# First q chunks copied out of PSUM before their rotation, their norms placed within later products, and some squares and weight sums on GpSimd

## Chip, cores and metric

The kernel runs on one core of a Trainium2 chip, as one program. The metric is the device time of that program in microseconds (us); lower is better. Engines are named as in the profile: TensorE (PE, with its weight loads as PEld), VectorE (DVE), ScalarE (ACT), GpSimd (POOL) and SyncE (SP, which issues the DMA transfers). Each engine works through its own list of instructions in a fixed order, and semaphores hold an instruction until what it needs is there.

## What is computed

A two-layer trunk over 1024 prompt frames and 32 sample frames, model width 1024: layer 0 mixes by retention, layer 1 by gated linear attention (GLA), each followed by a convolutional FFN (2 x 2816 wide), with RMS norms ahead of each part and a last norm. Cut to what the change touches:

```python
def rmsnorm(x, g):
    y = x * lax.rsqrt(jnp.mean(x * x, axis=-1, keepdims=True) + EPS)
    return y * g

def rotary(x, pos):                       # on q and k of each retention head
    x1, x2 = x[..., :half], x[..., half:]
    return concatenate([x1 * cos - x2 * sin, x1 * sin + x2 * cos])

def conv_ffn(h, conv_state, w_up, conv_w, conv_b, w_down):
    u = h @ w_up                          # then a causal convolution over 3 frames
    ...
    return (silu(gate) * val) @ w_down, ext[:, T:]

def trunk(...):
    for i in range(DEPTH):
        x = x + mixer(rmsnorm(x, norm_mix[i]))
        x = x + conv_ffn(rmsnorm(x, norm_ffn[i]), ...)
    return rmsnorm(x, norm_final), ...
```

## The kernel before

Everything is float32, kept transposed: features on the 128 partitions (eight tiles `kt`), frames along the free axis. A product of float32 values is made of three matmuls: each operand is split into a rounded high part and a low remainder (`hi`, `lo`; `whi` by a ScalarE cast at L102 and `wlo` by a VectorE subtraction at L103; for the activations `XA` at L146 on ScalarE and L147 on VectorE), and hi x hi, hi x lo and lo x hi add up in PSUM (L120, L121, L122). So each weight tile and each activation tile costs ScalarE one instruction and VectorE one before TensorE can use it.

The mixing parts work in three chunks of frames, `CM`: 384, 384 and 288 wide; the FFN's up-projection in four quarters of 264 (`TH`), two quarters to a half `s`.

**The start.** `retention()` (L258) loads the transposed input in three chunks `xc` and the first two weight tiles of head 0's q (`w01`). Then, for each chunk `c`: every `kt` is split (`split_x`, L144 to L147) and squared (`sumsq`, L126 to L142). The square is on ScalarE for even `kt` (L131) and on VectorE for odd `kt` (L129); the squares are added up in two `ss` tiles, on VectorE for even and on GpSimd for odd `kt` (L142), from a ring of two `sq` buffers. `rot_proj` makes the chunk's q in a PSUM pair `pj` (two of them exist). `rms_a` (L152) sums the squares over partitions (`pn`, L160), goes through a short chain of 128x3 operations (L167 to L172) and makes a diagonal matrix `dg` (L174); `rms_b` (L178) multiplies it by ones (`pr`, L180) and copies the row of reciprocal roots to `R` (L182, ScalarE). The norm is put into the rotation's factors: `cos` and `sin` of the chunk are multiplied by `R` (L312, L313, VectorE), and `rot` (L274) multiplies q, read from PSUM, by them (`tc` L281, `ts` L282, VectorE) and makes the rotated `qk` from those two on GpSimd (L284, L285). After the three chunks the pool `rp` is opened, `rotary(0, 1)` makes k of head 0 in the same way, and the loop over the nine blocks of 128 frames begins, with `pss` (L353) as its first matmul.

**The FFN.** `ffn_up` (L926) makes the up-projection in a scheme of seven products instead of eight for each pair of column tiles `f` (22 of them) and half `s`. Sums of activation blocks are made by `x_sums` (L906: `minus` at L918, the split at L913 on ScalarE and L914 on VectorE, into `XA` and `XB`), and sums of weight blocks by `weight_sums(f)` (L930): two tiles `rg` and `rv` are loaded, `rg` is split (`wgh`, `wgl`), and four additions or subtractions of 128x512 (L943, L944, L945, L949) and two more splits (`wsh`/`wsl`, `wth`/`wtl` at L938 on ScalarE, L939 on VectorE) follow; `wv` (L947, L948) splits one half of `rv`. Products (L987, L991, L992) leave PSUM by ScalarE copies (L966) and VectorE additions (L962). The first quarters' residual additions (L1115), norm (`pn`, `dg`, `pr` at L1126) and scaling by the norm (L1139) are still running on VectorE when `weight_sums(0)` and `weight_sums(1)` are made.

The instruction order of each engine is fixed when the program is built, by the order of the text and a scheduler that takes dependences and buffers into account; `order(ins, after)` adds a dependence without a wait, to hold an instruction behind another in that order.

Of the kernel before, what the change touches and what calls it, by code (L numbers as in the profile page):

```python
# [9 lines left out]
F32 = mybir.dt.float32  # L10
# [40 lines left out]
def trunk_kernel(ctx: ExitStack, tc: tile.TileContext, io):  # L51
# [63 lines left out]
    def proj(ps, w, c0, n):  # L115
        hi, lo = w
        for kt in range(KT):
            k = slice(kt * P, kt * P + P)
            rh = xh[:, kt, c0:c0 + n]
            PE.matmul(ps, hi[:, k], rh, start=kt == 0, stop=False)  # L120
            PE.matmul(ps, hi[:, k], xl[:, kt, c0:c0 + n], start=False, stop=False)  # L121
            PE.matmul(ps, lo[:, k], rh, start=False, stop=kt == KT - 1)  # L122

    def sumsq(ss, kt, src, n, on_dve=False):  # L126
        def square(dst):
            if on_dve:
                V.tensor_tensor(dst, src, src, op=ALU.mult)  # L129
            else:  # L130
                S.activation(dst, src, AF.Square)  # L131

        s_ = ss[kt % len(ss)]
        if kt < len(ss):
            square(s_[:, :n])
            if n < 384:
                G.memset(s_[:, n:], 1.0)
        else:
            sq = nps[0].tile([P, 384], F32, tag="sq", name=f"sq{uid()}", bufs=2)
            square(sq[:, :n])  # L140
            eng = V if kt % 2 == 0 else G
            eng.tensor_tensor(s_[:, :n], s_[:, :n], sq[:, :n], op=ALU.add)  # L142
# [34 lines left out]

    def rms_b(dg, c, ps, copy=True):  # L178
        c0, n = CM[c]
        PE.matmul(ps[:, :n], ones, dg.rearrange("p m t -> p (m t)")[:, :n], start=True, stop=True)  # L180
        if copy:
            S.copy(R[:, c0:c0 + n], ps[:, :n])  # L182

    def new_ss(depth=1):
        return [nps[0].tile([P, 384], F32, tag="ss", name=f"ss{uid()}", bufs=2 * depth) for _ in range(2)]
# [72 lines left out]
    def retention():  # L258
# [5 lines left out]
        def rsm(name):  # L264
            return pp.tile([P, 512], F32, tag="sm", name=name, bufs=2)

        def rot_proj(w, c):
            c0, n = CM[c]
            ps = pp.tile([P, 2, 512], F32, tag="pj", name=f"pj{uid()}", bufs=2)
            for d in range(2):  # L270
                proj(ps[:, d, :n], w[d], c0, n)
            return ps

        def rot(ps, c, j):  # L274
# [14 lines left out]
        with pool("x0", bufs=3, side="right") as xp, pool("x0n", side="right") as nps[0]:  # L289
            for c, (c0, n) in enumerate(CM):  # L290
                xc = xp.tile([P, KT, 384], F32, tag="xc", name=f"xc{c0}")
                step = 2 if c == 0 else 8
                for kt in range(0, KT, step):
                    nc.sync.dma_start(xc[:, kt:kt + step, :n], io["xT"][:, kt:kt + step, c0:c0 + n])
                    if c == 0 and kt in (0, 6):
                        w01.append(load_w(io["w_rqk"][0, kt // 6]))
                xs.append(xc)
            ones_ident()
            cos = const("cos", [P, T], pl=rk)
            sin = const("sin", [P, T], pl=rk)  # L300
            rmask = const("rmask", [P, RH, P], pl=rk)
            rcol = const("rcol", [P, RH, 4], pl=rk)
            qs0 = []
            for c, (c0, n) in enumerate(CM):
                ss = new_ss(2)
                for kt in range(KT):
                    split_x(0, xs[c][:, kt, :n], kt, c0, n)
                    sumsq(ss, kt, xs[c][:, kt, :n], n, kt % 2)
                ps = rot_proj(w01, c)
                dg = rms_a(ss, c, pp.tile([P, 512], F32, tag="sm", name=f"pn{uid()}", bufs=2), True)  # L310
                rms_b(dg, c, pp.tile([P, 512], F32, tag="sm", name=f"pr{uid()}", bufs=2))
                V.tensor_tensor(cos[:, c0:c0 + n], cos[:, c0:c0 + n], R[:, c0:c0 + n], op=ALU.mult)  # L312
                V.tensor_tensor(sin[:, c0:c0 + n], sin[:, c0:c0 + n], R[:, c0:c0 + n], op=ALU.mult)  # L313
                qs0.append(rot(ps, c, 0))
        rp = es.enter_context(pool("rp"))

        def rotary(h, j):
            w = [load_w(io["w_rqk"][h, 2 * j + d]) for d in range(2)]
            return [rot(rot_proj(w, c), c, j) for c in range(3)]

        def split_state(st):
            i = uid()
# [583 lines left out]
    def x_sums(X, x1, x2):  # L906
# [7 lines left out]
                V.tensor_tensor(X[o][:, 1], v, X[o][:, 0].bitcast(F32), op=ALU.subtract)  # L914
            return run

        def minus(d, a, b):
            return lambda: V.tensor_tensor(d, a, b, op=ALU.subtract)  # L918

        if x2 is None:  # L920
            return [split(1, b11), split(2, b21)]
        return ([minus(b12, b12, b11), split(5, b12)],
                [split(3, b22), minus(b22, b22, b12), split(6, b22),
                 minus(b11, b22, b11), split(7, b11), minus(b21, b22, b21), split(4, b21)])

    def ffn_up(l, X, todo, fc, sm, early, after):  # L926
        cw, cc, cst, room = fc
# [2 lines left out]
        def weight_sums(f):  # L930
# [9 lines left out]
                return h, l_  # L940

            g = split(rg, "wg")
            V.tensor_tensor(rv[:, a], rv[:, a], rv[:, b], op=ALU.add)  # L943
            V.tensor_tensor(rg[:, a], rv[:, a], rg[:, a], op=ALU.subtract)  # L944
            V.tensor_tensor(rg[:, b], rg[:, b], rg[:, a], op=ALU.subtract)  # L945
            v = w_tile(f"wv{uid()}")
            S.copy(v[:, a], rv[:, b])  # L947
            V.tensor_tensor(v[:, b], rv[:, b], v[:, a].bitcast(F32), op=ALU.subtract)  # L948
            V.tensor_tensor(rv[:, b], rv[:, b], rg[:, a], op=ALU.subtract)  # L949
            s2 = split(rg, "ws")  # L950
            s1 = split(rv, "wt")
            W[f] = {1: (g[0][:, a], g[1][:, a]), 2: (g[0][:, b], g[1][:, b]),
# [416 lines left out]
```

## Time and profile before

| | |
|---|---|
| time, median of 3 runs | 2928.82 us (2928.03 to 2929.93) |
| the profiled execution's own time | 2924.91 us |
| its span | 2923.1 us |
| mean granted TensorE clock | 0.995 |
| retention's first blocks begin (first L353) | 74.48 us |
| up-projection of the FFNs begins | about 944 us and 2184 us |

How to read it: times in a timeline are us from the start of the span; a row gives start, duration, engine, line, operation, `out<-in`, shapes, the count of instructions put together in the row, and in brackets the idle time before it with the instruction that ended it. Durations overlap somewhat within an engine: the next instruction of VectorE may start about 0.08 us before the last one ends, so what an instruction costs is the distance from its start to the next start. In a list of waits a row gives the waiting instruction, what it waited for, and the total, the number and the longest of the waits in us. A group gives its count, busy time and mean in ns of one, and then the idle time before it.

### The profile page before, as it was taken

What the parts mean: (1) busy time and instruction counts of PE and PEld (TensorE: products, weight loads), DVE (VectorE), ACT (ScalarE), POOL (GpSimd) and SP (SyncE); (2) the same over time, 40 slices, a digit from 0 to 9 for tenths busy, and PEclk for the clock granted to TensorE, in tenths of its full rate; (3) what the DMA queues carried; (4) which work ended last, traced back from release to release, by engine and by line L of the source; (5) the groups of instructions that cost most, each with busy time, mean ns of one, the idle gap of its engine ahead of it and who ended that gap; (6) DMA issues with size and microseconds to landing.
All of it is one profiled execution on the core that took longest, in us unless ns stands there. A gap on an engine that the chain in (4) does not pass through costs nothing.

```text
span 2923.1 us, 50853 instructions
## 1 busy us (share of the span) xinstructions
PE 2874.0 (98%) x20390; PEld 2776.0 (95%) x20390; DVE 1872.5 (64%) x3143; ACT 1248.0 (43%) x2238; POOL 328.9 (11%) x560
## 2 busy tenths in 40 slices
PE   8999999999999999999999999999999999999998
PEld 7888889899999999999999999999999999999998
DVE  7545464544477877777555577774488777775553
ACT  4424242422355444444444455553354444444443
POOL 3010101000011111111000032220010111110000
PEclk9999999999999999999999999999999999999999
DMA  4120211254656121222754401114642222227543
GB/s 153 37 88 28 86 57 57 90 173 164 217 183 213 59 87 72 84 79 75 260 181 170 166 21 50 50 43 152 216 155 73 81 74 82 73 86 242 183 161 125
DMA packets 168108, 339.69 MB, mean 116 GB/s; under 512 B 23712, under 2 KB 106784, under 8 KB 167872
## 3 DMA queue, kind: packets, MB, share of 16 engines
q1 hardware_dynamic: 167328, 335.87, 33.6%
q8 instruction: 159, 2.61, 0.4%
q14 instruction: 77, 0.63, 0.1%
q10 hardware_dynamic: 544, 0.59, 0.1%
HBM read 263.93 MB, written 72.47 MB: 115 GB/s over the span
## 4 chain that ended last, share of the span: by engine, by line
PE 90%; DVE 5%; ACT 2%; issue 1%; DMA 1%; POOL 1%; SPq 0%; DVEq 0%; ACTq 0%; POOLq 0%
PE pu L992 10%; PE pu L987 10%; PE pu L991 10%; PE pd L860 8%; PE pd L861 8%; PE pd L862 8%; PE pg L120 3%; PE pg L121 3%; PE pg L122 3%; PE pj L120 3%; PE pj L122 3%; PE pj L121 3%; PE psv L203 2%; PE psv L201 2%; PE psv L202 2%; PE pl L586 1%
## 5 line engine op out<-in xcount | busy, mean ns | idle before, releaser
L103 DVE TENSOR_TENSOR wlo<-raw,whi 128x1024 fp32r<-128x1024 f32 x258 | 324.8, 1260 | 283.4 <-ACT whi L102 277.4
L102 ACT CAST whi<-raw 128x1024 fp32r<-128x1024 f32 x258 | 269.9, 1049 | 482.2 <-PE pd L861 252.4
L860 PE MATMUL pd<-hh,whi 128*128 128x384 f32 (+1 forms) x880 | 284.7, 323 | 0.0
L862 PE MATMUL pd<-hh,wlo 128*128 128x384 f32 (+1 forms) x880 | 284.1, 323 | 0.0
L861 PE MATMUL pd<-hl,whi 128*128 128x384 f32 (+1 forms) x880 | 283.9, 323 | 0.1
L966 ACT COPY AR<-pu 128x264 f32<-128x264 f32 x264 | 99.1, 375 | 308.9 <-PE pu L992 306.5
L120 PE MATMUL pj<-XA,whi 128*128 128x384 f32 (+1 forms) x576 | 189.7, 329 | 11.4 <-ACT whi L102 7.4
L121 PE MATMUL pj<-XA,whi 128*128 128x384 f32 (+1 forms) x576 | 190.0, 330 | 2.4 <-DVE XA L147 2.2
L122 PE MATMUL pj<-XA,wlo 128*128 128x384 f32 (+1 forms) x576 | 188.4, 327 | 0.2 <-DVE wlo L103 0.2
L120 PE MATMUL pg<-XA,whi 128*128 128x352 f32 x576 | 186.0, 323 | 0.0
L121 PE MATMUL pg<-XA,whi 128*128 128x352 f32 x576 | 184.6, 320 | 0.0
L122 PE MATMUL pg<-XA,wlo 128*128 128x352 f32 x576 | 184.5, 320 | 0.0
L861 PEld LDWEIGHTS pd<-hl,whi 128*128 128x128 f32 x880 | 165.2, 188 | 0.8 <-DVE hl L837 0.4
L860 PEld LDWEIGHTS pd<-hh,whi 128*128 128x128 f32 x880 | 165.2, 188 | 0.5
L862 PEld LDWEIGHTS pd<-hh,wlo 128*128 128x128 f32 x880 | 165.2, 188 | 0.1
L860 PE MATMUL pd<-XB,whi 128*128 128x264 f32 x576 | 165.1, 287 | 0.0
L862 PE MATMUL pd<-XB,wlo 128*128 128x264 f32 x576 | 164.1, 285 | 0.0
L861 PE MATMUL pd<-XB,whi 128*128 128x264 f32 x576 | 164.0, 285 | 0.0
L1021 DVE SCALAR_TENSOR_TENSOR AR<-AR,cw 128x1058 f32<-128x1058 f32 x88 | 115.9, 1317 | 72.5 <-ACT AR L1020 72.5
L142 POOL TENSOR_TENSOR ss<-ss,sq 128x264 f32<-128x264 f32 (+2 forms) x48 | 50.8, 1058 | 929.3 <-ACT sq L131 906.7
L992 PE MATMUL pu<-XA,wgl 128*128 128x264 f32 x528 | 150.0, 284 | 0.0
L987 PE MATMUL pu<-XA,wgh 128*128 128x264 f32 x528 | 149.8, 284 | 0.0
(356 smaller groups left out, 9225.7 us busy)
## 6 DMA issues: line engine op xcount, KB each, us to landing
raw<-w_down SPq DMA_DIRECT2D x120, 512.0 KB, 3.6
raw<-w_ro SPq DMA_DIRECT2D x55, 512.0 KB, 3.8
rg<-w_up SPq DMA_DIRECT2D x44, 512.0 KB, 3.5
rv<-w_up SPq DMA_DIRECT2D x44, 512.0 KB, 3.4
scr_h<-AR SPq DMA_DIRECT2D x44, 512.0 KB, 2.6
AR<-scr_h SPq DMA_DIRECT2D x84, 192.0 KB, 3.8
raw<-w_go SPq DMA_DIRECT2D x23, 512.0 KB, 4.3
AR<-scr_or SPq DMA_DIRECT2D x16, 528.0 KB, 5.5
```

What stands on the lines that cost most here:

```text
L102: S.copy(hi, raw)
L103: V.tensor_tensor(lo, raw, hi.bitcast(F32), op=ALU.subtract)
L120: PE.matmul(ps, hi[:, k], rh, start=kt == 0, stop=False)
L121: PE.matmul(ps, hi[:, k], xl[:, kt, c0:c0 + n], start=False, stop=False)
L122: PE.matmul(ps, lo[:, k], rh, start=False, stop=kt == KT - 1)
L860: PE.matmul(o, w[0][:, k], h[0][:, :n], start=i == 0, stop=False)
L861: PE.matmul(o, w[0][:, k], h[1][:, :n], start=False, stop=False)
L862: self.last_mm = PE.matmul(o, w[1][:, k], h[0][:, :n], start=False, stop=i == nk - 1)
L987: mm = PE.matmul(ps, wh[:, k], x[:, 0, kt], start=m in (1, 2, 4, 5) and kt == 0, stop=False, skip_group_check=True)
L991: PE.matmul(ps, wh[:, k], x[:, 1, kt], start=False, stop=False, skip_group_check=True)
L992: mm = PE.matmul(ps, wl[:, k], x[:, 0, kt], start=False, stop=kt == 3, skip_group_check=True)
L1021: V.scalar_tensor_tensor(cj, uj[:, 1:T + 3], cw[:, nt, 1:2], cj, op0=ALU.mult, op1=ALU.add)
```

## The change

Three edits.

1. In the start, each of the first three q chunks is copied from PSUM, unrotated, by ScalarE into an SBUF tile. The norm of chunk c is made within the product of chunk c + 1 (`norm_first` after the first half, `norm_last` after the second, held there with `order`), and that of chunk 2 within the first chunk of k, which is projected before the pool `rp` is opened (`ahead_k`). The rotation reads the SBUF copy.
2. `sumsq` in these three chunks makes the squares of odd `kt` on GpSimd instead of VectorE. (Its other callers do not pass the argument.)
3. In the FFN, the four weight sums of `f` = 0 and 1 are made on GpSimd, and the subtraction that makes `b21` also, which is moved ahead of the split of product 6.

```diff
             PE.matmul(ps, hi[:, k], xl[:, kt, c0:c0 + n], start=False, stop=False)
-            PE.matmul(ps, lo[:, k], rh, start=False, stop=kt == KT - 1)
+            mm = PE.matmul(ps, lo[:, k], rh, start=False, stop=kt == KT - 1)
+        return mm
...
-    def sumsq(ss, kt, src, n, on_dve=False):
+    def sumsq(ss, kt, src, n, on_pool=False):
         def square(dst):
-            if on_dve:
-                V.tensor_tensor(dst, src, src, op=ALU.mult)
+            if on_pool:
+                G.tensor_tensor(dst, src, src, op=ALU.mult)
             else:
                 S.activation(dst, src, AF.Square)
...
     def rms_b(dg, c, ps, copy=True):
         c0, n = CM[c]
-        PE.matmul(ps[:, :n], ones, dg.rearrange("p m t -> p (m t)")[:, :n], start=True, stop=True)
+        mm = PE.matmul(ps[:, :n], ones, dg.rearrange("p m t -> p (m t)")[:, :n], start=True, stop=True)
         if copy:
             S.copy(R[:, c0:c0 + n], ps[:, :n])
+        return mm
...
-        def rot_proj(w, c):
+        def rot_proj(w, c, last_norm=False):
             c0, n = CM[c]
             ps = pp.tile([P, 2, 512], F32, tag="pj", name=f"pj{uid()}", bufs=2)
             for d in range(2):
-                proj(ps[:, d, :n], w[d], c0, n)
+                mm = proj(ps[:, d, :n], w[d], c0, n)
+                if last_norm:
+                    (norm_last if d else norm_first)(2, mm)
             return ps
...
+            stage = {}
+
+            def norm_first(c, after):
+                stage[c] = rms_a(stage[c], c, rsm(f"pn{uid()}"), True, after)
+
+            def norm_last(c, after):
+                c0, n = CM[c]
+                order(rms_b(stage[c], c, rsm(f"pr{uid()}")), after)
+                V.tensor_tensor(cos[:, c0:c0 + n], cos[:, c0:c0 + n], R[:, c0:c0 + n], op=ALU.mult)
+                V.tensor_tensor(sin[:, c0:c0 + n], sin[:, c0:c0 + n], R[:, c0:c0 + n], op=ALU.mult)
+                qs0[c] = rot(qs0[c], c, 0)
+
             for c, (c0, n) in enumerate(CM):
-                ss = new_ss(2)
+                stage[c] = new_ss(2)
                 for kt in range(KT):
                     split_x(0, xs[c][:, kt, :n], kt, c0, n)
-                    sumsq(ss, kt, xs[c][:, kt, :n], n, kt % 2)
-                ps = rot_proj(w01, c)
-                dg = rms_a(ss, c, pp.tile([P, 512], F32, tag="sm", name=f"pn{uid()}", bufs=2), True)
-                rms_b(dg, c, pp.tile([P, 512], F32, tag="sm", name=f"pr{uid()}", bufs=2))
-                V.tensor_tensor(cos[:, c0:c0 + n], cos[:, c0:c0 + n], R[:, c0:c0 + n], op=ALU.mult)
-                V.tensor_tensor(sin[:, c0:c0 + n], sin[:, c0:c0 + n], R[:, c0:c0 + n], op=ALU.mult)
-                qs0.append(rot(ps, c, 0))
+                    sumsq(stage[c], kt, xs[c][:, kt, :n], n, kt % 2)
+                ps = pp.tile([P, 2, 512], F32, tag="pj", name=f"pj{uid()}", bufs=2)
+                mm = proj(ps[:, 0, :n], w01[0], c0, n)
+                if c:
+                    norm_first(c - 1, mm)
+                mm = proj(ps[:, 1, :n], w01[1], c0, n)
+                q = rk.tile([P, 2, 384], F32, tag="qk0", name=f"qk{uid()}", bufs=3)
+                S.copy(q[:, :, :n], ps[:, :, :n])
+                qs0.append(q)
+                if c:
+                    norm_last(c - 1, mm)
+            wk = [load_w(io["w_rqk"][0, 2 + d]) for d in range(2)]
+            ahead_k = [(wk, rot_proj(wk, 0, True))]
         rp = es.enter_context(pool("rp"))

         def rotary(h, j):
-            w = [load_w(io["w_rqk"][h, 2 * j + d]) for d in range(2)]
-            return [rot(rot_proj(w, c), c, j) for c in range(3)]
+            w, ps = ahead_k.pop(0) if h == 0 else ([load_w(io["w_rqk"][h, 2 * j + d]) for d in range(2)], None)
+            return [rot(ps if ps and c == 0 else rot_proj(w, c), c, j) for c in range(3)]
...
-        def minus(d, a, b):
-            return lambda: V.tensor_tensor(d, a, b, op=ALU.subtract)
+        def minus(d, a, b, eng=V):
+            return lambda: eng.tensor_tensor(d, a, b, op=ALU.subtract)
...
-                [split(3, b22), minus(b22, b22, b12), split(6, b22),
-                 minus(b11, b22, b11), split(7, b11), minus(b21, b22, b21), split(4, b21)])
+                [split(3, b22), minus(b22, b22, b12), minus(b21, b22, b21, G), split(6, b22),
+                 minus(b11, b22, b11), split(7, b11), split(4, b21)])
...
-            V.tensor_tensor(rv[:, a], rv[:, a], rv[:, b], op=ALU.add)
-            V.tensor_tensor(rg[:, a], rv[:, a], rg[:, a], op=ALU.subtract)
-            V.tensor_tensor(rg[:, b], rg[:, b], rg[:, a], op=ALU.subtract)
+            E = G if f < 2 else V
+            E.tensor_tensor(rv[:, a], rv[:, a], rv[:, b], op=ALU.add)
+            E.tensor_tensor(rg[:, a], rv[:, a], rg[:, a], op=ALU.subtract)
+            E.tensor_tensor(rg[:, b], rg[:, b], rg[:, a], op=ALU.subtract)
...
-            V.tensor_tensor(rv[:, b], rv[:, b], rg[:, a], op=ALU.subtract)
+            E.tensor_tensor(rv[:, b], rv[:, b], rg[:, a], op=ALU.subtract)
```

In the changed kernel the lines move: the scheme's first matmul `pss` is L377 there, L120 to L122 stay.

## Prediction

> **What bounds the kernel now.** I read the page first, its busy shares and the chain that ended last.
>
> ```profile
> span 2923.1 us, 50853 instructions
> PE 2874.0 (98%) x20390; PEld 2776.0 (95%) x20390; DVE 1872.5 (64%) x3143; ACT 1248.0 (43%) x2238; POOL 328.9 (11%) x560
> PE 90%; DVE 5%; ACT 2%; issue 1%; DMA 1%; POOL 1%; SPq 0%; DVEq 0%; ACTq 0%; POOLq 0%
> ```
>
> TensorE is busy for all but 49 us, and the change takes no matmul away (it issues the same 19308 TensorE rows in another order). It can therefore win only where TensorE waits. Busy time by stretch (us; busy of PE, PEld, DVE, ACT, POOL; the granted clock is the third column from the right) shows where that is, inside the two regions that the diff touches:
>
> ```profile
> 10.00:20.00 10.00, 7.87 (x37) 6.82 (x37) 10.00 (x15) 6.54 (x13) 4.37 (x3) 1.00 1.07 364
> 20.00:30.00 10.00, 9.03 (x54) 8.35 (x53) 8.83 (x20) 6.72 (x17) 4.45 (x5) 1.00 0.53 202
> 30.00:40.00 10.00, 8.26 (x47) 7.06 (x46) 10.00 (x21) 2.04 (x4) 3.89 (x4) 0.95 0.07 15
> 40.00:50.00 10.00, 8.14 (x41) 7.69 (x39) 9.35 (x11) 2.37 (x3) 6.94 (x7) 0.71 0.11 36
> 50.00:60.00 10.00, 10.00 (x59) 9.65 (x59) 7.70 (x15) 4.45 (x10) 2.77 (x2) 1.00 0.65 222
> 960.00:975.00 15.00, 12.52 (x94) 11.54 (x94) 13.77 (x17) 8.44 (x11) 0.00 (x0) 1.00 0.11 36
> 2170.00:2190.00 20.00, 17.03 (x135) 16.38 (x133) 18.65 (x37) 10.46 (x18) 2.73 (x3) 1.00 0.59 207
> ```
>
> From 10 to 50 us VectorE is busy 10.0, 8.83, 10.0 and 9.35 of each 10 us and TensorE never full: the start is bound by VectorE. After 50 TensorE is full. In 40 to 50 the clock is 0.71, so the waits there are paid twice. The two FFN windows say the same: TensorE short, VectorE at 13.77 of 15 and 18.65 of 20. The list of TensorE's waits between 7 and 80 us names the late work:
>
> ```profile
> PE pj L121 <- DVE XA L147: 2.2, 7, 0.7
> PE pj L120 <- DVE ts L282: 1.9, 1, 1.9
> PE pn L160 <- DVE ss L142: 1.6, 1, 1.6
> PE pr L180 <- DVE dg L174: 0.9, 1, 0.9
> ```
>
> These are 6.6 us that the change can aim at, all VectorE's; the clock's 0.71 over 10 us adds at most 2.9. So 9.5 us is the ceiling of the start.
>
> **The start, part by part.** (a) The square of every odd kt, four per chunk, goes from VectorE to GpSimd. What does VectorE save, and what does a GpSimd instruction cost it? The timeline (start, us, engine, line) has both:
>
> ```profile
> 10.02 0.55 DVE L129 TENSOR_TENSOR sq<-xc 128x384 f32<-128x384 f32 x1
> 10.49 0.62 DVE L147 SCALAR_TENSOR_TENSOR XA<-xc,gcol,XA 128x384 fp32r<-128x384 f32 x1
> 11.49 1.37 DVE L147 SCALAR_TENSOR_TENSOR XA<-xc,gcol,XA 128x384 fp32r<-128x384 f32 x1
> 27.23 1.35 DVE L147 SCALAR_TENSOR_TENSOR XA<-xc,gcol,XA 128x384 fp32r<-128x384 f32 x1
> 36.70 0.45 DVE L129 TENSOR_TENSOR sq<-xc 128x288 f32<-128x288 f32 x1
> ...
> 10.65 1.79 POOL L142 TENSOR_TENSOR ss<-ss,sq 128x384 f32<-128x384 f32 x1 [10.21 <-DVE sq L129]
> 25.86 2.31 POOL L142 TENSOR_TENSOR ss<-ss,sq 128x384 f32<-128x384 f32 x1 [2.05 <-DVE rc L172]
> 61.82 1.01 POOL L284 TENSOR_TENSOR qk<-tc,ts 128x384 f32<-128x384 f32 x1 [2.65 <-DVE ts L282]
> ```
>
> A square holds VectorE from 10.02 to 10.49, 0.47 us, 0.08 less than its duration (so 0.37 at 288). The removed squares give 8 x 0.47 + 4 x 0.37 = 5.2 us. But the same L147 takes 0.62 us alone and 1.37 or 1.35 while a GpSimd instruction runs (10.65 to 12.44, 25.86 to 28.17). So a GpSimd instruction lengthens one VectorE instruction by about 0.75, and is itself stretched from 1.01 (at 61.82, VectorE idle) to 1.79 or 2.31. If all twelve new ones meet such an instruction, VectorE pays 12 x 0.75 = 9.0 us, net +3.8 in the stretch it bounds; if none does, it gains 5.2. I take nearly all meeting one, since VectorE is 88 to 100% busy there. The Trainium skill's page "SBUF — State Buffer", section "Who interferes with whom", says that a VectorE instruction reading two SBUF operands and a GpSimd one that reads SBUF exclude each other wholly. The trace agrees that they exclude each other, but at a smaller size, 0.75 us of a 1.01 us instruction; by the page's size the sum would be rival 2's.
>
> (b) q leaves PSUM by a ScalarE copy (128x768 twice, 128x576 once) instead of two VectorE products. No such copy is in the trace; the nearest rows are these:
>
> ```profile
> L182 ACT COPY R<-pr 128x384 f32<-128x384 f32 x2 | 1.0, 479 | 2.6 <-PE pr L180 2.6
> L102 ACT CAST whi<-raw 128x1024 fp32r<-128x1024 f32 x9 | 9.3, 1045 | 16.7 <-PE pj L121 16.6
> L281 DVE TENSOR_TENSOR tc<-pj,cos 128x768 f32<-128x768 f32 x4 | 3.8, 952 | 8.0 <-PE pj L122 6.6 <-POOL qk L285 1.4
> ```
>
> Between 0.48 and 1.05 I take 0.8, by elements. ScalarE is 65 to 67% busy from 10 to 30, so its time is covered, but its place is not: the copy of chunk 0 waits for that chunk's last matmul and stands ahead of chunk 1's L146 casts from kt 3 on, which TensorE needs. In the same queue the squares of even kt now share the two sq buffers with GpSimd's, so ScalarE waits for GpSimd's adds eight times in the scheduled order, ahead of the second whi cast. (c) The norms of chunk c - 1 stand within chunk c's product and the rotations (2 x 0.95 each) behind it, off the saturated stretch; a PSUM pair is free after 0.8 us and not after norm, cos, sin, tc and ts. That removes the 1.9 and most of the 1.6 above. The rotation now reads SBUF twice, so it too meets GpSimd. (d) k's two weight loads and its first chunk are emitted before the pool of the heads is opened; SP issues the same loads, and DMA is 11% busy from 40 to 50, so they cost nothing; without that cover one costs about 3.8 us (raw loads' landing).
>
> Walking the scheduled order with these durations, each engine in order and each GpSimd instruction charged 0.75 to VectorE: kt 7 of chunk 0 starts at 18.5, against 16.85 now; chunk 0's product ends at 24.3, against 21.5; chunk 2's at 47.4, against 49.8 (the norm's pn begin where a product ends):
>
> ```profile
> 16.85 0.44 PE L121 MATMUL pj<-XA,whi 128*128 128x384 f32 x1
> 21.52 1.17 PE L160 MATMUL pn<-ones,ss 128*128 128x1 f32 x10
> 49.80 1.17 PE L160 MATMUL pn<-ones,ss 128*128 128x1 f32 x10
> 45.79 4.97 DVE L103 TENSOR_TENSOR wlo<-raw,whi 128x1024 fp32r<-128x1024 f32 x3
> 74.48 0.61 PE L353 MATMUL pss<-qk,qk 128*128 128x128 f32 x4
> ```
>
> So 2.8 us is lost on chunk 0 and 5.2 won back over chunks 1 and 2: 2.4 ahead. What is late next is chunk 1's pr: its dg stands on VectorE behind the first rotation and the wlo of k's weights (three take 4.97 us at 45.79), and by the walk comes at 53.1, inside k's first product, where TensorE arrives at 49.7 and its whole queue stands for 3.4 us. That turns 2.4 ahead into 1.0 behind; chunk 2's norm, now made inside the same product, waits for its own small operations for 0.7 more: k's products end 1.7 us after today's 74.48. Bounds: without any GpSimd charge, and dg early, 6 us earlier; with the clock lowered behind that gap as in 40 to 50, 4 later. I take +1.7.
>
> **The FFNs.** For f = 0 and 1 four 128x512 sums go to GpSimd in each FFN, and one 128x1056 difference (L918, b21) twice per FFN, the second ahead of split 6. GpSimd rows of these widths are missing; from 0.76 at 264 and 1.01 at 384, 2.1 ns an element, I estimate 1.3 and 2.4 us, and the charge to VectorE in the ratio 0.75 to 1.01: 1.0 and 1.8 to 2.1. VectorE saves at most the 0.68 (at 2181.93) and 1.25 that its own take.
>
> ```profile
> 944.55 0.76 POOL L142 TENSOR_TENSOR ss<-ss,sq 128x264 f32<-128x264 f32 x1 [39.48 <-ACT sq L131]
> 968.88 1.25 DVE L918 TENSOR_TENSOR AR<-AR 128x1056 f32<-128x1056 f32 x1
> PE pu L991 <- DVE XB L914: 1.4, 2, 1.2
> PE pu L987 <- ACT XB L913: 1.1, 2, 0.7
> ...
> 2179.62 1.22 DVE L939 TENSOR_TENSOR wgl<-rg,wgh 128x1024 fp32r<-128x1024 f32 x1
> 2181.93 0.68 DVE L943 TENSOR_TENSOR rv<-rv 128x512 f32<-128x512 f32 x1
> 2187.05 1.04 DVE L944 TENSOR_TENSOR rg<-rv,rg 128x512 f32<-128x512 f32 x1
> 2189.10 1.04 ACT L938 CAST wsh<-rg 128x1024 fp32r<-128x1024 f32 x1 [0.79 <-DVE rg L945]
> PEld pu L987 <- ACT wsh L938: 2.9, 1, 2.9
> PE pr L1126 <- DVE dg L174: 1.3, 2, 0.9
> ```
>
> In the first FFN TensorE waits 2.5 us from 960 on for the splits L914 and L913. The difference L918 costs VectorE about 0.8 more on GpSimd than it saves there, in the stretch that sets these waits; and GpSimd's sum for f = 1, waiting for its load, stands ahead of the add L142 of 944.55, whose sq buffer ScalarE's next square and an eviction behind it need: about 1 us. The sums of f = 0 end over 9 us ahead of use and save nothing. I take +1.5 of -1 (the moved difference is hidden) to +3.
>
> In the second FFN the 2.9 us wait is for wsh, whose sums L944 and L945 stand on VectorE behind evictions, and wsh is cast at 2189.10. On GpSimd they may start when wgl has read rg, at 2180.8, and end near 2183.5; ScalarE's squares, which wait for GpSimd's adds, hold the cast until about 2187.5: 1.5 of the 2.9 is saved. The sums of f = 1 leave the chain to the last dg, 1 to 1.5 less; the difference costs 0.8 again. I take -2, of -5 (all three waits gone) to +2 (GpSimd's first difference holds VectorE ahead of evictions).
>
> **Sum.** +1.7 + 1.5 - 2 = +1.2 us on the profiled execution's 2924.91, that is 2926.1. The runs shown have 2928.82, 3.9 us above it, so the median comes out at 2930.0.
>
> **The rivals.** (1) Faster: GpSimd's charges fall where VectorE would wait anyway, dg comes early, and the start keeps 5 of its 6 us, the second FFN its 4, the first +0.5: -8.5, 2920.3. For it: ScalarE's copy does free PSUM early, and the wsh wait has one clear cause. Against: no GpSimd instruction in 10 to 50 leaves VectorE unharmed in the timeline. (2) Slower, by one mechanism: GpSimd excludes VectorE for its whole instruction, not for 0.75 of it. Then a 384 square costs 1.0, a difference 2.4; the start gets 12 x 0.25 = 3 us more, the FFNs 4 x 0.5 and 16 x 0.3 of which the half lies in bound stretches, 3.4: +7.6, 2936.4. It decides once chunk 2's product ends later than today's 49.8. For it: 25.86's 2.31 us beside L147 and dg; against: 1.37 - 0.62 = 0.75 at 11.49. The Trainium skill's page "Perfetto Trace Analysis", section "Optimizing Scalar/DVE Operations", warns that moving work from VectorE to GpSimd may not help, as they share a read port; that is this rival, and (a) its measured half. (3) The change is inert in the FFNs, ScalarE's casts keeping their places: +1.7 alone, 2930.5, not to be told from the forecast.
>
> **How the numbers follow.** A measurement of this kernel tells about 0.2%, 5.9 us, from no change: 2923.0 to 2934.7 counts as same. The forecast with (3) has 0.42, rival 1 0.30, rival 2 0.28. The forecast's tails reach over both bounds with 0.04 each, and a tenth of each rival falls back within: faster 0.27 + 0.04 = 0.31, slower 0.25 + 0.04 = 0.29, same the other 0.40. The range reaches a little beyond both rivals, leaving out what lies past all bounds at once: 2919 to 2938; the forecast's own is 2925 to 2935.
>
> **What would show it.** Right: VectorE's 384 instructions near 1.3 us beside GpSimd's squares; chunk 0's kt 7 at 18 to 19; a TensorE wait for dg of 2 to 5 us in k's first product; first L353 (then L377) at 75 to 78; the 2.9 us wait for wsh halved. Wrong: that matmul before 72 (then the charges are hidden or dg is early), or after 79; a clock below 0.9 in 50 to 60, where it is 1.00 now; GpSimd's 512 rows over 2 us.

## The result, and the profile after

The changed kernel takes 2950.14 us, the median of five runs (2949.45 to 2956.93), against 2928.82 for the kernel before (five runs, 2924.4 to 2929.93). The ratio is 1.0082, 95% interval 1.0068 to 1.0096: slower by 20 to 28 us, where 2930.0 was predicted, in a range of 2919 to 2938, and its dearest case gave 2936.4. The profiled execution of the changed kernel took 2952.39 us. From its page, the span, the busy shares and the chain that ended last by engine:

```profile
span 2950.1 us, 50884 instructions
PE 2892.2 (98%) x20390; PEld 2790.5 (95%) x20390; DVE 1868.6 (63%) x3111; ACT 1249.6 (42%) x2241; POOL 380.6 (13%) x592
PE 87%; DVE 5%; ACT 2%; issue 2%; POOL 1%; DMA 1%; DVEq 0%; SPq 0%; POOLq 0%; ACTq 0%
```

VectorE did 4 us less work, as meant, and GpSimd 52 more. The totals don't say where 27 us of span went (the two medians lie 21 us apart; some 6 us of the 27 are the scatter of the two executions profiled). Both traces hold 20390 matmul records, so the start of the n-th (counted from 0) can be compared, and the lag read off at the borders of the regions. Layers are numbered 0 and 1; the "gate's down-projection" is the product `pd` with the weights `w_ro` or `w_go` that closes a layer's mixing part, and the "head" of an up-projection is its first stretch, where the sums for the seven products are made:

| up to matmul | where | before, us | lag of after, us | added here |
|---|---|---|---|---|
| 230 | start, k of head 0 | 58.96 | 3.95 | +4.0 |
| 5000 | retention, unchanged | 869.53 | 4.21 | +0.3 |
| 5300 | layer 0, gate's down-projection | 906.52 | 9.12 | +4.9 |
| 5900 | layer 0, head of the up-projection | 983.83 | 13.56 | +4.4 |
| 14600 | rest of the FFN, GLA, unchanged | 2132.46 | 14.36 | +0.8 |
| 14950 | layer 1, gate's down-projection | 2176.58 | 20.08 | +5.7 |
| 15300 | layer 1, head of the up-projection | 2229.38 | 25.94 | +5.9 |
| 20389 | rest, unchanged | 2915.94 | 27.03 | +1.1 |

The start lost 4.0 where 1.7 was predicted; the first FFN with its down-projection 9.3 where 1.5 was; the second 11.6 where a gain of 2 was. So it is the FFN term that failed, and half of its loss lies in a stretch, the down-projections, that the sum did not contain.

How far one execution scatters can be read from the kernels run later. Those whose FFNs are as before (s_alone, q_alone, s_late, sq_late, sq_late_dg, sq_start) move by -0.8 to +0.4 us in a down-projection, by 0.0 to 0.8 in the first head and by 0.2 to 2.4 in the second, so the last head's 5.9 is uncertain by some 2 us. Nine kernels with the start as before have their first pss between 74.22 and 76.75, on average at 75.1; three with the changed start whole have it at 78.56, 78.73 and 79.03. The start's loss is thus nearer 3.7 than 4.1 us.

The start first. Busy time by stretch of the changed kernel (columns as before: PE, PEld, DVE, ACT, POOL, then the granted clock), and TensorE's waits between 7 and 85 us:

```profile
10.00:20.00 10.00, 7.39 (x23) 5.06 (x22) 10.00 (x10) 4.94 (x9) 8.77 (x8) 0.84 1.06 364
20.00:30.00 10.00, 9.09 (x38) 7.88 (x36) 4.97 (x7) 3.75 (x8) 2.66 (x3) 0.82 0.53 202
30.00:40.00 10.00, 8.89 (x30) 8.18 (x31) 7.82 (x14) 5.27 (x13) 5.79 (x8) 0.52 0.07 16
40.00:50.00 10.00, 10.00 (x68) 9.73 (x68) 10.00 (x17) 5.73 (x10) 5.25 (x8) 0.96 0.15 53
PE pj L121 <- DVE XA L148: 4.3, 7, 1.6
PE pr L181 <- DVE dg L175: 1.4, 1, 1.4
```

VectorE, the bound of this stretch before, is now busy 4.97 of 10 us in 20 to 30, and the clock has fallen to 0.52 in 30 to 40: TensorE looks busy at half speed. The timeline says what VectorE waited for:

```profile
25.54 0.80 ACT L333 COPY qk<-pj 128x768 f32<-128x768 f32 x1 [8.36 <-PE pj L122]
26.79 0.56 DVE L143 TENSOR_TENSOR ss<-ss,sq 128x384 f32<-128x384 f32 x1 [5.03 <-ACT sq L132]
55.05 0.89 PE L181 MATMUL pr<-dg,ones 128*128 128x384 f32 x2 [1.39 <-DVE dg L175]
78.56 0.61 PE L377 MATMUL pss<-qk,qk 128*128 128x128 f32 x4
```

ScalarE's copy of chunk 0 is the row to look at: 0.80 us of work, and 8.36 us in which ScalarE's queue stood for the end of that chunk's product, with chunk 1's squares and its casts from kt 3 on behind it. VectorE then had nothing to do for 5.03 us, and TensorE came into chunk 1 with only the first three of its eight tiles cast.

The FFN regions, from the timeline of the same execution:

```profile
875.89 5.71 POOL L942 TENSOR_TENSOR AR<-AR 128x1056 f32<-128x1056 f32 x1 [16.03 <-DVE AR L942]
876.86 1.26 DVE L942 TENSOR_TENSOR AR<-AR 128x1056 f32<-128x1056 f32 x1
878.03 1.26 DVE L938 TENSOR_TENSOR XA<-AR,XA 128x1056 fp32r<-128x1056 f32 x1
881.63 2.05 ACT L937 CAST XA<-AR 128x1056 fp32r<-128x1056 f32 x2 [3.77 <-POOL AR L942]
882.74 2.43 DVE L938 TENSOR_TENSOR XA<-AR,XA 128x1056 fp32r<-128x1056 f32 x2 [3.46 <-ACT XA L937]
892.18 1.05 ACT L102 CAST whi<-raw 128x1024 fp32r<-128x1024 f32 x1 [5.97 <-DMA raw<-w_ro]
902.91 0.36 PE L884 MATMUL pd<-XB 128*128 128x264 f32 x1 [2.56 <-DVE AR L1140]
976.93 2.43 POOL L942 TENSOR_TENSOR AR<-AR 128x1056 f32<-128x1056 f32 x1 [13.40 <-DVE AR L942]
977.10 3.37 DVE L942 TENSOR_TENSOR AR<-AR 128x1056 f32<-128x1056 f32 x1
2169.41 4.93 POOL L942 TENSOR_TENSOR AR<-AR 128x1056 f32<-128x1056 f32 x1 [12.30 <-DVE AR L942]
2174.38 1.07 ACT L937 CAST XA<-AR 128x1056 fp32r<-128x1056 f32 x1 [3.94 <-POOL AR L942]
2177.78 0.43 DVE L143 TENSOR_TENSOR ss<-ss,sq 128x264 f32<-128x264 f32 x1 [4.08 <-ACT sq L132]
2178.61 0.59 PE L884 MATMUL pd<-XB 128*128 128x264 f32 x1 [3.32 <-DVE AR L1140]
2200.20 3.74 POOL L968 TENSOR_TENSOR rv<-rv 128x512 f32<-128x512 f32 x1 [11.69 <-DMA rv<-w_up]
2210.61 0.39 PE L1012 MATMUL pu<-XA,wsh 128*128 128x264 f32 x1 [2.45 <-ACT AR L991]
```

The difference of 128x1056 takes 5.71 us on GpSimd at 875.89 and 4.93 at 2169.41, not the 2.4 of the estimate, and VectorE's instructions beside the first are not lengthened at all (1.26 each): here GpSimd is the one that waits, until VectorE stops for other reasons (its last instruction ends at 879.29, the difference 2.3 us later; at 2169.41 VectorE turns to its evictions, which read PSUM, at 2171.93, and the difference ends 2.4 us later). ScalarE's cast for the split of the first block stands in its queue and waits 3.77 for GpSimd, VectorE 3.46 for ScalarE; the next raw weights are late, and ScalarE waits 5.97 for them at 892.18; and TensorE, some 20 us on, waits 2.56 for an eviction.

In layer 1's down-projection the way is shorter: the cast waits 3.94 for GpSimd, ScalarE's squares stand behind the cast, VectorE's addition of the squares waits 4.08 for them with evictions behind it, and TensorE waits 3.32 for one of these. No load of raw weights is issued or waited for between 2160 and 2182.

At 976.93 GpSimd came first: it takes 2.43, and VectorE's own L942 takes 3.37 instead of 1.25, 2.12 more. In layer 1's head the first weight sum takes 3.74 us on GpSimd (2200.20), and TensorE waits 2.45 for a ScalarE copy (2210.61).

### The profile page after: what moved, and what is told of

It reads as the page before. It is cut to its first block, busy times and chain, and to the rows that moved or that the text cites. A ratio compares the mean times of both kernels' runs of the same rounds, so it can differ in the third digit from the quotient of the medians.

```text
span 2950.1 us, 50884 instructions
## 1 busy us (share of the span) xinstructions
PE 2892.2 (98%) x20390; PEld 2790.5 (95%) x20390; DVE 1868.6 (63%) x3111; ACT 1249.6 (42%) x2241; POOL 380.6 (13%) x592
## 4 chain that ended last, share of the span: by engine, by line
PE 87%; DVE 5%; ACT 2%; issue 2%; POOL 1%; DMA 1%; DVEq 0%; SPq 0%; POOLq 0%; ACTq 0%
PE pu L1017 10%; PE pu L1012 10%; PE pu L1016 10%; PE pd L884 7%; PE pd L885 7%; PE pd L886 7%; PE pg L120 3%; PE pg L121 3%; PE pg L122 3%; PE pj L122 3%; PE pj L120 3%; PE pj L121 3%; PE psv L205 2%; PE psv L203 2%; PE psv L204 2%
## 5 line engine op out<-in xcount | busy, mean ns | idle before, releaser
L120 PE MATMUL pj<-XA,whi 128*128 128x384 f32 (+1 forms) x576 | 191.4, 333 | 8.0 <-ACT whi L102 7.1
L122 PE MATMUL pj<-XA,wlo 128*128 128x384 f32 (+1 forms) x576 | 190.1, 330 | 0.4 <-DVE wlo L103 0.3
L120 PE MATMUL pg<-XA,whi 128*128 128x352 f32 x576 | 186.0, 323 | 0.0
L122 PE MATMUL pg<-XA,wlo 128*128 128x352 f32 x576 | 184.5, 320 | 0.0
L987 DVE TENSOR_TENSOR AR<-AR,pu 128x264 f32<-128x264 f32 (+2 forms) x440 | 145.3, 371 | 7.2 <-PE pu L1017 7.1
```

The costliest lines, as they stand in the source:

```text
L122: mm = PE.matmul(ps, lo[:, k], rh, start=False, stop=kt == KT - 1)
L987: V.tensor_tensor(u[:, d:d + n], t[:, o:o + n], b[:, o:o + n], op=op)
```

## The experiments

Every kernel is an edit of the kernel before or of the changed one. Times are medians with the ratio to the kernel before, run beside it.

| label | what is in it | median, us | ratio, 95% interval |
|---|---|---|---|
| s_alone | copies and moved norms | 2927.71 | 0.9998, 0.9989 to 1.0008 |
| q_alone | squares on GpSimd | 2929.88 | 1.0004, 0.9994 to 1.0013 |
| b_alone | difference b21 on GpSimd, earlier | 2946.98 | 1.0060, 1.0041 to 1.0079 |
| w_alone | weight sums of f = 0, 1 on GpSimd | 2931.43 | 1.0012, 1.0002 to 1.0021 |
| b_place | difference earlier, on VectorE | 2926.76 | 1.0002, 0.9991 to 1.0012 |
| b_all | difference and its split on GpSimd | 2949.35 | 1.0075, 1.0060 to 1.0090 |
| w_f1 | sums of f = 1 only | 2928.91 | 1.0005, 0.9995 to 1.0015 |
| w_ordered | sums; casts behind the squares | 2934.95 | 1.0022, 1.0011 to 1.0033 |
| no_b | whole change but the difference | 2936.18 | 1.0027, 1.0017 to 1.0037 |
| sq_start | the changed start alone | 2933.54 | 1.0012, 1.0002 to 1.0022 |
| ctl_r4w9 | before, 4 raw and 9 split buffers | 2950.52 | 1.0070, 1.0053 to 1.0087 |
| b_r4w9 | that with the difference on GpSimd | 2952.96 | 1.0076, 1.0058 to 1.0093 |
| s_late | copies later in ScalarE's queue | 2926.99 | 0.9996, 0.9987 to 1.0004 |
| sq_late | that with squares on GpSimd | 2926.23 | 0.9994, 0.9984 to 1.0003 |
| sq_late_dg | and rotations behind the next dg | 2921.30 | 0.9979, 0.9970 to 0.9988 |

**The four parts, one at a time.** s_alone is the changed kernel with `V.tensor_tensor` for the square, `E = V`, and the old list in `x_sums`; the others put one part into the kernel before (cut to the lines that matter):

```diff
 # q_alone, in sumsq
-                V.tensor_tensor(dst, src, src, op=ALU.mult)
+                G.tensor_tensor(dst, src, src, op=ALU.mult)
 # b_alone, in x_sums
-                [split(3, b22), minus(b22, b22, b12), split(6, b22),
-                 minus(b11, b22, b11), split(7, b11), minus(b21, b22, b21), split(4, b21)])
+                [split(3, b22), minus(b22, b22, b12), minus(b21, b22, b21, G), split(6, b22),
+                 minus(b11, b22, b11), split(7, b11), split(4, b21)])
 # w_alone, in weight_sums: the four sums on E
+            E = G if f < 2 else V
```

> Only the start is restructured (q copied by ScalarE, norms within later products); squares stay on VectorE, the FFNs are as before. If GpSimd's squares are what makes the start late (theory A), the first pss matmul comes 2 to 6 us before today's 74.48, and the time is 2 to 6 us below the kernel before. If the copies and the reordered queues make it late (rival), the first pss comes at 77 to 79, as in the changed kernel (78.56), and the time is 3 to 5 us above.

> Only the squares of odd kt in the start go to GpSimd, the rest is as before. Theory A: the first pss at 78 to 81, from 12 GpSimd instructions that each hold VectorE for about 0.75 us, less 5.2 us of squares removed, and from ScalarE's squares that wait for GpSimd's adds; time 4 to 6 us above before. Rival: the first pss within 1 us of 74.48, no change in time.

> Only the difference that makes b21 goes to GpSimd and ahead of the split of product 6. Theory B (ScalarE's cast of that block stands ahead of others in its fixed order and waits for a GpSimd instruction of 2.4 to 5.7 us, and everything behind it in ScalarE's queue is late): 4 to 6 us lost in each gate's down-projection and 2 to 3 in the second half of each FFN's sums, 12 to 16 us in all. Rival (only VectorE's own time counts, 2.1 us of exclusion against 1.17 saved, four times): 3 to 4 us in all.

> Only the weight sums of f = 0 and 1 go to GpSimd. Theory C (the sums are early, but ScalarE's cast of wsh then stands ahead of its squares and waits for a weight buffer that TensorE still reads, so squares, norm and an eviction are late): the 2.9 us wait for wsh goes, a wait of TensorE of 2 to 3 us for a ScalarE copy comes in its place, and the time is 0 to 4 us above before. Rival (the prediction's step: 1.5 us of that wait and 1 us of the norm chain are saved): 2 to 3 us below.

By the ratios the parts are -0.6, +1.2, +17.6 and +3.5 us, together 21.7, near the whole's 0.0082 x 2928 = 24. The intervals of the first two contain 1; the difference's reaches from 12 to 23 us. The difference is some three quarters of the loss. Its trace repeats the rows above:

```profile
878.49 2.05 ACT L913 CAST XA<-AR 128x1056 fp32r<-128x1056 f32 x2 [3.75 <-POOL AR L918]
889.45 1.05 ACT L102 CAST whi<-raw 128x1024 fp32r<-128x1024 f32 x1 [6.39 <-DMA raw<-w_ro]
900.70 0.56 PE L860 MATMUL pd<-XB 128*128 128x264 f32 x1 [3.38 <-DVE AR L1115]
```

By matmul counts it loses 6.6 and 4.2 us in the two down-projections and 3.0 and 5.0 in the two heads. The rival, VectorE's own time alone, gave 3 to 4. The first pss of s_alone comes at 74.77 and of q_alone at 76.75, against 74.48:

```profile
74.77 0.61 PE L377 MATMUL pss<-qk,qk 128*128 128x128 f32 x4
```

```profile
76.75 0.61 PE L353 MATMUL pss<-qk,qk 128*128 128x128 f32 x4
```

Neither was as early, or as late, as theory A expected. The copies alone are not the gain that it promised. What the squares alone cost is not shown: w_f1 below, whose start is as before, has its first pss at 76.75 too (w_f1's clock from 40 to 50 us was 0.55, that of the kernel before 0.71), and the time of q_alone can't be told from no change.

**Place or engine, and which queue.** b_place moves the difference as the change does, but on VectorE. b_all has the difference as in b_alone and puts the cast and the subtraction of product 4's split on GpSimd too:

```diff
-                S.copy(X[o][:, 0], v)
-                V.tensor_tensor(X[o][:, 1], v, X[o][:, 0].bitcast(F32), op=ALU.subtract)
+                if o == 4:
+                    G.tensor_copy(X[o][:, 0], v)
+                else:
+                    S.copy(X[o][:, 0], v)
+                (G if o == 4 else V).tensor_tensor(X[o][:, 1], v, X[o][:, 0].bitcast(F32), op=ALU.subtract)
```

> The difference b21 stands ahead of the split of product 6 but stays on VectorE. If the engine is the cause (theory B), the time is within 2 us of before; if its place is (rival: it delays the split of product 6 by its own 1.17 us, four times, and what waits for that), 4 to 6 us above.

> As in the kernel with the difference on GpSimd, and the cast and the subtraction that split b21 for product 4 are on GpSimd too, so ScalarE waits for no difference and GpSimd has twelve 128x1056 operations instead of four. Theory B (ScalarE's queue behind the cast): the 4 to 5 us lost in the first layer's gate down-projection go to under 1.5; in the second layer part of the loss stays, since GpSimd's adds for the squares queue behind three operations there; in all +5 to +12 instead of +18. Rival (GpSimd excluding VectorE is the loss): three times as many operations, three times the loss, over +30 in all.

The place costs nothing (0.0002), so it is the engine. b_all lost 22 us and fits neither theory: more than theory B's 12, less than the rival's 30. Its first down-projection lost more than b_alone's, 8.1 us against 6.6, though ScalarE waited for no difference. Its timeline, and one row of TensorE's waits, show another way to the same end:

```profile
875.45 3.46 DVE L917 TENSOR_TENSOR XA<-AR,XA 128x1056 fp32r<-128x1056 f32 x1
881.19 3.47 DVE L103 TENSOR_TENSOR wlo<-raw,whi 128x1024 fp32r<-128x1024 f32 x1
890.88 1.05 ACT L102 CAST whi<-raw 128x1024 fp32r<-128x1024 f32 x1 [10.59 <-DMA raw<-w_ro]
PE pd L860 <- DVE AR L1118: 5.8, 1, 5.8
```

VectorE is shut out for 2.2 us twice (3.46 and 3.47 instead of 1.25 and 1.22), wlo is late, and so is the next load of raw weights, for which ScalarE then waits 10.59 us. Theory B in its narrow form, ScalarE's cast, is not the only way: whatever delays wlo does it, since a raw buffer (there are three) is free only behind its wlo. The traces show this link: in the kernel before a wlo ends at 880.06 and SyncE issues the next load at 880.09; in b_alone these are 883.51 and 883.53.

**The raw buffers.** That was tried by a fourth. It takes the place of one of the ten buffers of split weights, so a control has the same two numbers without the difference on GpSimd:

```diff
-        return wp.tile([P, D], F32, tag="raw", name=name, bufs=3)
+        return wp.tile([P, D], F32, tag="raw", name=name, bufs=4)
-        return wp.tile([P, D], F32R, tag="w", name=name, bufs=10)
+        return wp.tile([P, D], F32R, tag="w", name=name, bufs=9)
```

> The kernel before with four buffers for raw weights instead of three, and nine for split weights instead of ten: the control for the next run. Within 5 us of before, either way.

> That control with the difference b21 on GpSimd. If the loss in the gate down-projections goes through the raw weight buffers (late wlo on VectorE, so the next load starts late, so evictions behind its wlo are late), a fourth buffer takes most of the 5 to 6 us away in each: +6 to +10 us against the control instead of +18. If the loss is ScalarE's and VectorE's queues alone (rival), it stays at +15 to +20.

The control itself lost 20 us, far from the 5 expected: by matmul counts, nine buffers of split weights cost about 10 us spread over each up-projection. Against it the difference on GpSimd costs 0.0006, about 2 us, instead of 17.6, less than the 6 to 10 expected; the two intervals leave this uncertain by some 7 us either way. ScalarE's first long wait for raw weights, 6.39 us in b_alone, is gone, although the difference still takes 4.54 us on GpSimd there. That cast, then TensorE's waits from 860 to 915 us, of b_r4w9 and then of its control:

```profile
887.67 1.05 ACT L102 CAST whi<-raw 128x1024 fp32r<-128x1024 f32 x1 [0.88 <-PE pd L861]
PE pd L860 <- DVE AR L1115: 1.7, 2, 1.2
```

```profile
PE pd L860 <- DVE AR L1115: 0.9, 1, 0.9
```

By matmul counts the first down-projection loses 1.0 there (b_alone 6.6). So the raw ring carries the loss in that one. The second loses 0.7 (4.2), but this says nothing of the ring: its difference takes only 2.59 us in b_r4w9, and in b_alone the loss went through the squares and evictions (ScalarE's cast waits 3.94, VectorE's addition of squares 4.08, TensorE 3.4), with no load of raw weights between 2159 and 2181. In the head of the first up-projection 2.7 of 3.0 us are still lost: there it is the exclusion (VectorE's difference takes 3.47 us at 967.40 in b_r4w9) and the cast behind it. The head of the second gains 1.0 against the control: the same exclusion is there, but an earlier wait of TensorE is 2.2 us instead of the control's 4.3.

**The weight sums.**

```diff
 # w_f1
+            E = G if f == 1 else V
 # w_ordered: w_alone, and in weight_sums' split, for f = 0 (last_sq is ScalarE's last square)
+                if f == 0 and name != "wg":
+                    order(cast, last_sq[0])
```

> Only the weight sums of f = 1 go to GpSimd. Theory C (the loss comes from f = 0, whose wsh cast stands ahead of ScalarE's squares): no loss, -1 to +1 us, with today's 2.9 us wait for wsh still there. Rival (the sums of f = 1 are at fault, stretching the 128x3 operations of the last norm to over 1 us): +2 to +4.

> The weight sums of f = 0 and 1 on GpSimd, and the casts of wsh and wth of f = 0 held behind ScalarE's last square of the down-projection before. Theory C: squares and the first evictions are on time again, the waits of TensorE near the first wsh together under 1.5 us, and the time 0 to 4 us below before. Rival (the sums themselves, through their exclusion of VectorE, cost it): 3 to 5 us above before, as with the sums alone.

w_f1 loses nothing that can be told (1.0005), which points to f = 0, as theory C says, though its interval and that of w_alone overlap. The cause read from the traces is not the one theory C gave. Of w_alone, the first sum, ScalarE's cast and TensorE's wait (a row of its list of waits):

```profile
2182.84 4.39 POOL L944 TENSOR_TENSOR rv<-rv 128x512 f32<-128x512 f32 x1 [11.54 <-DVE XA L914]
2190.00 1.05 ACT L938 CAST wsh<-rg 128x1024 fp32r<-128x1024 f32 x1 [6.14 <-POOL rg L946]
PE pu L988 <- ACT wth L938: 5.2, 1, 5.2
```

and of w_ordered, where ScalarE's squares come first:

```profile
2183.08 4.99 POOL L947 TENSOR_TENSOR rv<-rv 128x512 f32<-128x512 f32 x1 [10.81 <-DMA rv<-w_up]
2192.99 0.73 ACT L131 ACTIVATE sq<-AR 128x264 f32<-128x264 f32 x2 [4.26 <-POOL ss L142]
PE pu L991 <- ACT AR L970: 4.7, 1, 4.7
```

The first sum takes 4.39 or 4.99 us, against 1.29 for the next, because VectorE runs from one SBUF subtraction to the next beside it: it ends 1.24 us after VectorE turns to its evictions (2185.99 in w_alone, 2186.83 in w_ordered). Then either the cast waits for the sums, with the squares behind it, or the squares wait for GpSimd's adds L142, which stand behind the sums in GpSimd's own queue. Order on ScalarE does not mend that: w_ordered, with 1.0022 (6 us), was no faster than w_alone and above the 3 to 5 us of its rival.

**From the other side.** no_b is the changed kernel with the difference back; sq_start is its start with the old FFNs.

> The changed kernel with only the difference b21 back on VectorE and in its old place. If its move is most of the loss, as alone (+18 of +21), the time is 2 to 7 us above before. If it costs that much only alone and the parts overlap (rival), 10 us or more stay.

> The changed start whole (copies, norms moved, squares on GpSimd), the FFNs as before. The copies and norms alone gave the first pss 0.3 us late, the squares alone 2.3 us. If the two only add, 77.0 to 77.5 and +1 to +3 us in the time; if they hinder each other (ScalarE's queue now waits for GpSimd's adds and holds the copies and casts, and the clock falls in the longer gaps, as in the changed kernel), 78 to 79 and +3 to +5 us.

Without the difference 0.0027 stays, so it costs 0.0055, 16 us, in the whole as well; what stays, 8 us, is a little over the 2 to 7 expected. sq_start has the first pss at 78.73, more than 0.3 + 2.3 late: copies and squares hinder each other.

**The start's queue orders.** s_late and sq_late emit each copy after the next chunk's splits and hold it there; sq_late_dg also emits cos, sin and the rotation of chunk c after the norm of chunk c + 1:

```diff
 # s_late (squares on VectorE) and sq_late (on GpSimd)
                     sumsq(stage[c], kt, xs[c][:, kt, :n], n, kt % 2)
+                if c:
+                    copy_q(c - 1)      # S.copy, with order(copy, last_cast) for c < 2
 # sq_late_dg, in norm_first; finish has cos, sin and rot
                 stage[c] = rms_a(stage[c], c, rsm(f"pn{uid()}"), True, after)
+                if c:
+                    finish(c - 1)      # order(cos and sin, last_dg) for c < 2
```

> The start with copies and moved norms, squares on VectorE, and the copies of chunks 0 and 1 held in ScalarE's queue behind the casts of the next chunk. If the place of the copies costs the start (ScalarE stood 8.36 us for the copy of chunk 0 in the changed kernel, with the next casts and squares behind it), the first pss comes at 70 to 73 and the time is 2 to 4 us below before, faster than both kernels. If VectorE's work bounds the start all the same (rival), the first pss stays at 74 to 75.5 and the time within 1.5 us of before.

> The same with the squares of odd kt on GpSimd. If the copies' place is what the changed start lost, the first pss falls from 78.7 to 74 to 76; if GpSimd's squares and adds are (ScalarE waiting for the sq buffers, VectorE excluded), it stays at 77.5 to 79.

> As sq_late, and the rotations of chunks 0 and 1 (cos, sin, tc, ts) held on VectorE behind the next chunk's dg. In sq_late the clock and the wait of TensorE for that dg cost 4.5 us after it had stood 4.7 ahead of before. If VectorE's order is what delays dg, that wait falls under 0.5 us, the first pss comes at 69 to 71 and the time is 3 to 6 us below before. If dg waits for its own chain (rival), the first pss stays at 73 to 74 and the time within 2 us of before.

The first pss of sq_start, sq_late and sq_late_dg:

```profile
78.73 0.61 PE L377 MATMUL pss<-qk,qk 128*128 128x128 f32 x4
```

```profile
46.93 1.65 PE L182 MATMUL pr<-dg,ones 128*128 128x384 f32 x2 [2.12 <-DVE dg L176]
73.72 0.61 PE L387 MATMUL pss<-qk,qk 128*128 128x128 f32 x4
```

```profile
70.59 0.61 PE L398 MATMUL pss<-qk,qk 128*128 128x128 f32 x4
```

The copies' place is worth 5.0 us with GpSimd's squares, and almost nothing without them (s_late at 74.64, a miss): with the squares still on VectorE it is VectorE that bounds, as s_late's list of TensorE's waits has it:

```profile
PE pj L121 <- DVE XA L148: 6.3, 3, 2.8
```

With GpSimd's squares, sq_late's first pss is 0.9 us ahead of s_late's, which is within the scatter: they at least do no harm there. The order behind dg is worth another 3.1 us (4 by the ratios). From sq_late_dg, TensorE's wait for dg and two stretches:

```profile
PE pr L183 <- DVE dg L177: 0.3, 1, 0.3
30.00:40.00 10.00, 9.55 (x62) 8.72 (x60) 8.65 (x17) 7.05 (x15) 7.28 (x12) 1.00 0.07 16
40.00:50.00 10.00, 10.00 (x68) 9.68 (x68) 9.46 (x15) 4.58 (x7) 2.70 (x2) 1.00 0.51 163
```

TensorE is full from 40 to 70, at clock 1.00 where it was 0.71 from 40 to 50 before. sq_late_dg, with the changed start and none of the FFN's parts, is faster than both kernels: 0.21% below the one before.

## Why the prediction was wrong

Point by point, by its own steps. (The 19308 TensorE rows that it names stand in no trace; both traces hold 20390 matmul records. Nothing in its sum rests on them.)

- **The FFNs, first: "the difference L918 costs VectorE about 0.8 more on GpSimd than it saves there".** This is the step that failed. It priced the move as VectorE's time, in the heads of the up-projections alone. b_alone measured 17.6 us, more than half of it in the down-projections, where two of the four differences stand and where the sum had no term but an upper bound of +2 for the second FFN. What was missed is who waits: the cast in ScalarE's fixed order, and behind it, in layer 0, wlo on VectorE and the three raw buffers, in layer 1, the squares and the evictions. b_place shows the engine to be the cause, b_r4w9 the ring in layer 0; the way in layer 1 is read from the trace, and no run tested it.
- **Its size was wrong as well.** 2.4 us was estimated by the widths; 2.43 was measured where GpSimd came first, 5.71 and 4.93 where VectorE was running without a gap. The rows quoted for the price (0.75 us to VectorE, GpSimd stretched to 2.31) already had both directions in them, and only one was carried on. The 0.62 us at 10.49 that it took for VectorE alone stands beside GpSimd's add of 10.65 to 12.44: there VectorE was first.
- **The FFNs, second: "1.5 of the 2.9 is saved".** Wrong in sign. The sums were to start at 2180.8 and end at 2183.5. In w_alone the third of them, for which the cast waits, starts at 2188.68, the cast comes at 2190.00 instead of 2189.10, and TensorE waits 5.2 us instead of 2.7 (2.9 by its weight loads). The gain from f = 1, 1 to 1.5 us, is not seen in w_f1 (1.0005), whose interval goes no lower than -1.5 us.
- **The start: +1.7.** Right in sign and in its places, too small. The walk had chunk 0's kt 7 at 18.5 (17.72 measured) and dg of chunk 1 late by VectorE's queue (1.39 us of wait where 3.4 were walked; sq_late_dg shows that the order was its cause). The copy's place in ScalarE's queue was named, but no time was given to it: sq_late measures 5.0 us. That the loss came out at the bound of +4, set for a lowered clock, is luck: the bound had the clock low behind the wait for dg, and from 50 to 60 us it was 1.00; it was low from 10 to 40, ahead of it.
- **The squares, "net +3.8":** not borne out. q_alone's 2.3 us are within the scatter of one execution, and once the copies stand right the squares cost nothing that can be seen (sq_late against s_late). The exclusion is real (1.18 to 1.36 us for VectorE's 384-wide instructions that take 0.56 to 0.61 alone, near the charge of 0.75), but VectorE had room for it once nothing in the queues held it: 8.65 of 10 us busy from 30 to 40 in sq_late_dg, where it was 10.00 before.
- **The rivals.** Slower was the right side, with 0.29, but by exclusion alone it gave 2936.4. Its sign in the start came (the copy of chunk 2, which waits for that product, starts at 51.42, later than 49.8), but not by its mechanism: the charge there was the forecast's, and ScalarE's queue made the delay. The prediction's own sign against it, GpSimd rows of 512 over 2 us, came with 3.74. The Trainium skill's page "SBUF — State Buffer", section "Who interferes with whom", also says that the one that issues first takes the shared ports for its whole instruction, so that order decides who blocks. These traces agree: 2.12 us more on VectorE beside GpSimd's 2.43 in one place, 5.71 on GpSimd in another.

Left open: how the 5.9 us in the head of the second up-projection divide; b_alone and w_alone lost 5.0 and 2.9 there, kernels with unchanged FFNs up to 2.4, and one profiled execution of each does not tell them apart. A raw ring of four with all ten split buffers was not run.

## What to carry to other kernels

Price a moved instruction by every queue that waits for its result, not by the engine that is relieved: in-order queues turn one slow operation into a late cast, a late buffer and a late load. An operation on GpSimd has two durations, one alone and one beside a VectorE that runs without a gap, and a consumer ahead of urgent work has to be priced by the longer. When a part of a change is right in idea but loses, look at where its instructions landed in the queues: the same start went from 4 us late to 4 early by order alone.

## What was not expected of the hardware

The clock fell without a long stop. In the changed start no wait of TensorE between 10 and 50 us was over 1.60 us, yet the granted clock was 0.82 from 20 to 30 and 0.52 from 30 to 40, where short waits followed one another; sq_late_dg, with 0.79 from 20 to 30, was back at 1.00 in 30 to 50. The clock also differs between executions of the same start: from 40 to 50 it was 0.71 in the kernel before and 0.55 in w_f1. And a GpSimd instruction can wait very long for VectorE: a copy of 128x2 took 12.03 us in the kernel before,

```profile
871.73 12.03 POOL L977 COPY AR<-cc 128x2 f32<-128x2 f32 x1 [16.07 <-DVE AR L918]
```

while VectorE ran from one two-operand instruction into the next, without a gap until 883.71. That row was in the profile before the prediction was made; it was the one that told of the 5.71.
